# A hybrid decoder trunk on one core: the mixing stage in source order, taps on VectorE alone, seven W_out chunks open in PSUM

## The chip, the cores and the metric

The kernel runs on one core of a Trainium2 chip. The metric is the device time of one execution in microseconds. The engines are TensorE (PE, with its weight loads as PEld), VectorE (DVE), ScalarE (ACT), GpSimd (POOL) and SyncE (SP), which here only issues DMAs. Each engine and each DMA queue works off its own list of instructions in order.

## What is computed

Two layers over 512 positions of 1024 channels in float32; cut to what matters:

```python
def mixing_layer(h, ...):
    u = h @ w_in                       # 1024 -> 256+256+256+512+512+512+512
    a_b, a_c, a_x, q, k, v, c_in = split(u)
    y_a = a_b * causal_depthwise_conv(a_c * a_x, short_conv_w)        # 3 taps
    q, k = apply_rope(q), apply_rope(k)                                # 4 heads x 2 maps x 64
    o = diff_attention(q, k, v, lam)   # (softmax_1 - lam * softmax_2) v, causal
    y_b = rmsnorm(o, diff_subln_g) * (1.0 - lam_init)
    c = (c_in + glu_b); c = c[..., :256] * sigmoid(c[..., 256:])
    c = causal_depthwise_conv(c, conf_dw_w) + conf_dw_b                # 31 taps
    y_c = silu(layernorm(c, conf_ln_g, conf_ln_b))
    return concat([y_a, y_b, y_c]) @ w_out

for l in range(2):
    x = x + mixing_layer(rmsnorm(x, mix_norm_g[l]), ...)
    x = x + swiglu(rmsnorm(x, ffn_norm_g[l]), w_gate[l], w_up[l], w_down[l])   # hidden 2816
return rmsnorm(x, final_norm_g)
```

## The kernel before

The state `x` lies transposed in SBUF, as eight chunks of 128 channels x 512 positions. Every operand of a product is held as a rounded high part and a low part (fp32r), and a product is three matmuls, hi*hi, hi*lo and lo*hi (`mm3`, lines 152 to 154). The norm's scale `r` is applied after the projections, so that matmuls can start before it is known (`make_r`).

Weights come in units of eight 128x128 blocks (512 KB, 96 units a layer), in the order in which they are used. `prep` handles half a unit: the first half starts the unit's load on the SP queue (`raw`, two buffers), ACT makes the high part (line 125), and DVE or GpSimd subtracts it from the raw weights to get the low part (line 127; in the first 30 units of a layer two halves in three go to GpSimd). `next_half` prepares five halves ahead of the one in use; there are six tiles `w`.

The mixing stage of a layer: `conf_in` computes the gated columns `cc` (eight halves); `rotated(g, ...)` computes q and k of two heads (four units), rotates them with `cosr` and `sinr`, splits them and copies them with 64 KB DMAs on the SP queue into the packed tiles `pq`, `pk` (line 356): 16 copies for q and 32 for k of each pair of heads. `values` computes v for all heads into four PSUM banks (eight halves), and ACT evacuates it (`vt`, line 370). `Head.weigh` computes the scores of one block of 128 queries in both maps, their maxima (line 399), exponentials (line 401) and their combination (lines 404 to 406); `turn` transposes it through PSUM (line 416) and ACT copies it (line 418); `values` multiplies it with v (line 430); `finish` normalizes and transposes a head. `conf_conv` does the 31 taps of two chunks: 23 as one DVE operation each (lines 483 and 485), eight as a product on ACT and an addition on GpSimd (lines 488 to 493). `short_conv` is the gated convolution, `conf_out` the LayerNorm with its Silu. `stream` multiplies with W_out in two passes: first six of the eight inputs, then the last two (`YORDER`, `YCUT`), each pass adding its eight output chunks to `x`; the second pass also makes the next `h` and the sum of squares.

The order of the instructions of every engine and of SP's DMAs is chosen by the framework's planner from the program and its estimated times, not by the source: the source's order is a priority.

Of the kernel before, what the change touches and what calls it, by code (L numbers as in the profile page):

```python
# [43 lines left out]
POOL_TAPS = 8  # L44
# [11 lines left out]
YORDER = [6, 7, 2, 3, 0, 1, 4, 5]  # L56
YCUT = 6
# [17 lines left out]
def trunk(ctx, tc, xT, pos, wu, cv, lamv, cst, out):  # L75
# [13 lines left out]
    pc = pool("pc", 3)  # L89
# [3 lines left out]
    sc = pool("sc", 4, space=PSUM)  # L93
# [13 lines left out]
    def prep(i):  # L107

        if i >= 2 * L * UNITS or i in wtiles:
            return  # L110
        u, half = divmod(i, 2)
        if u not in wraw:
            wraw[u] = pw.tile([P, 2, 4 * P], F32, tag="raw", name=f"raw{u}", bufs=2)
            if u:
                nc.sync.dma_start(wraw[u].rearrange("p a b -> p (a b)"), wu[u])
            else:
                for j in range(2):
                    nc.sync.dma_start(wraw[u][:, j, :], wu[u, :, 4 * P * j:4 * P * j + 4 * P])
                    if j == 0:
                        nc.sync.dma_start(x[0], xT[0])  # L120
                        nc.sync.dma_start(cvt, cv)
# [46 lines left out]
    def four(name):  # L168
        return [sc.tile([P, S], F32, tag="sc", name=f"{name}{i}") for i in range(4)]
# [17 lines left out]
    prep(0)  # L187
    for k in range(1, KC):
        nc.sync.dma_start(x[k], xT[k])
        if k % 2 and k + 1 < AHEAD:  # L190
            prep(k)
            prep(k + 1)
    for i in range(1, AHEAD):
        prep(i)
# [25 lines left out]
    def add_square(k, run, eng):  # L220
        if k == 0:
            run = pt.tile([P, S], F32, tag="t", name="run")
            A.activation(run, x[0], AF.Square)
            return run
        sq = pt.tile([P, S], F32, tag="t", name="sq")
        A.activation(sq, x[k], AF.Square)
        (V if k == KC - 1 else eng).tensor_add(run, run, sq)
        return run
# [19 lines left out]
    def scale_of(parts, mul, eps, key, pool, ptag, n=4):  # L248
# [22 lines left out]
        if n < 4:  # L271
            dgs = [(diag(pe, a, F32, "at", V, bufs=3), ones_d)]
# [12 lines left out]
    def make_r(run):  # L285
        y, pb = scale_of([run], 1.0, RMS_EPS, "r", tp, "tp")
        rT = sm.tile([P, 4], F32, tag="rT", name="rT", bufs=2)
        V.tensor_scalar(rT, y, RQ, None, ALU.mult)
        r = cp.tile([P, S], F32, tag="r", name="r")
        A.copy(r, pb)  # L290
        return r, rT


    def rope_tables():
        p1, p2, p3 = _parts()
        pi = pt.tile([P, P], I32, tag="t", name="posi")
        A.dma_start(pi, pos)
# [19 lines left out]
        for b in range(4):  # L317
            A.dma_start(dr[:, :, b, :], tab[32 * b:32 * b + 32, :, :])
# [3 lines left out]
    def rotated(g, h, cosr, sinr):  # L322
# [3 lines left out]
        packs = []  # L326
        for isk in (False, True):
            ps = [unit(h, "qk") for _ in range(2)]
            t = [pt.tile([P, S], F32, tag="t", name=f"ro{i}") for i in range(4)]
            V.tensor_mul(t[0], ps[0], cosr)  # L330
            V.tensor_mul(t[1], ps[0], sinr)
            V.tensor_mul(t[2], ps[1], sinr)
            V.tensor_mul(t[3], ps[1], cosr)
            V.tensor_sub(t[0], t[0], t[2])
            V.tensor_add(t[1], t[1], t[3])
            for ab in range(2):
                o = t[ab]
                hl = pr.tile([P, 2, S], F32R, tag="hl", name="hl")
                if isk:
                    A.copy(hl[:, 0, :], o)  # L340
                    V.tensor_sub(hl[:, 1, :], o, hl[:, 0, :].bitcast(F32))
                else:
                    A.mul(hl[:, 0, :], o, QS)
                    V.scalar_tensor_tensor(hl[:, 1, :], o, QS, hl[:, 0, :].bitcast(F32), ALU.mult, ALU.subtract)
                if not packs:
                    packs += [[pk.tile([P, 2, S], F32R, tag=tag, name="p" + tag) for tag in ("q", "k1", "k2")]
                              for _ in range(2)]
# [9 lines left out]
        return packs  # L357

    def values(h, rT):
        ws = four("v")  # L360
        for k, b, w in side_by_side(3):
# [3 lines left out]
            T.matmul(ws[b], lhsT=h[k][:, 1, t], rhs=w[:, 0, :], start=False, stop=k == KC - 1)  # L365
        vt = []
# [7 lines left out]
    class Head:  # L374


        def __init__(self, hh, packs, nlam, gsub):
            self.hh, self.packs, self.nlam, self.gsub = hh, packs, nlam, gsub
            self.lsum = sm.tile([P, 2, 4], F32, tag="lsum", name="lsum")
            self.ss = sm.tile([P, 4], F32, tag="ss", name="ss")  # L380
            self.e, self.at = {}, {}
            self.o = self.raw = None

        def weigh(self, qb):

            q, k1, k2 = self.packs
            lsum = self.lsum
            n = (qb + 1) * P
            qs = slice(qb * P, n)
            e = []  # L390
            pss = [sc.tile([P, S], F32, tag="sc", name="ps") for _ in range(2)]
            for m in range(2):
                T.matmul(pss[m][:, :n], lhsT=q[:, m, qs], rhs=k1[:, m, :n], start=True, stop=False)
                T.matmul(pss[m][:, :n], lhsT=q[:, m, qs], rhs=k2[:, m, :n], start=False, stop=False)
                T.matmul(pss[m][:, qs], lhsT=idr, rhs=maskr, start=False, stop=True)
            for m in range(2):
                ps = pss[m]
                nm = sm.tile([P, 1], F32, tag="nm", name="nm")
                V.tensor_reduce(nm, ps[:, :n], AX.X, ALU.max, negate=True)
                t = pe.tile([P, S], F32, tag="e", name="e")  # L400
                A.activation(t[:, :n], ps[:, :n], AF.Exp, bias=nm, accum_out=lsum[:, m, qb:qb + 1])
                e.append(t)
            c = sm.tile([P, 1], F32, tag="c", name="c")
            V.reciprocal(c, lsum[:, 1, qb:qb + 1])
            V.tensor_scalar(c, c, lsum[:, 0, qb:qb + 1], self.nlam, ALU.mult, ALU.mult)
            V.scalar_tensor_tensor(e[0][:, :n], e[1][:, :n], c, e[0][:, :n], ALU.mult, ALU.add)
            self.e[qb] = e[0]

        def turn(self, qb):

            n = (qb + 1) * P
            e = self.e.pop(qb)
            pT = tp.tile([P, S], F32, tag="tp", name="pT")
            for kb in range(qb + 1):
                ks = slice(kb * P, kb * P + P)
                T.transpose(pT[:, ks], e[:, ks], ident)
            at = pe.tile([P, S], F32, tag="at", name="at", bufs=3)
            A.copy(at[:, :n], pT[:, :n])
            self.at[qb] = at

        def values(self, qb, vt):
            if qb == 0:
                self.o = av.tile([P, 4, P], F32, tag="av", name="o")
                self.raw = pe.tile([P, 4, P], F32, tag="os", name="os", bufs=2)
            o = self.o[:, qb, :]
            at = self.at.pop(qb)
            es = slice(self.hh * P, self.hh * P + P)
            for kb in range(qb + 1):
                ks = slice(kb * P, kb * P + P)
                T.matmul(o, lhsT=at[:, ks], rhs=vt[kb][:, es], start=kb == 0, stop=kb == qb)  # L430
            junk = sm.tile([P, P], mybir.dt.bfloat16, tag="junk", name="junk", bufs=1)
            A.activation(junk, o, AF.Square, accum_out=self.ss[:, qb:qb + 1])
            A.copy(self.raw[:, qb, :], o)

        def finish(self):

            e1 = sm.tile([P, 4], F32, tag="e1", name="e1")
# [3 lines left out]
            y0 = rsqrt(e1, 4, "h")  # L441
            raw = self.raw
            for qb in range(4):
# [406 lines left out]
```

## Time and profile before

| | us |
|---|---|
| median of 3 runs (1200.77 to 1202.13) | 1200.81 |
| the profiled execution | 1200.55 |
| its span, from first to last instruction | 1198.4 |
| PE busy in the span | 1146.2 |
| DVE busy in the span | 702.3 |
| mean granted TensorE clock, as a share of full speed | 0.981 |

A duration in the profile includes an instruction's way through the engine. Matmuls overlap: one of 128x512 is shown with 0.39 us, though the next one starts 0.227 us later; so a stage is measured by starts, idle time and granted clock. "idle before" in a row is the engine's idle time ahead of that instruction, with the instruction that ended it.

### The profile page before, as it was taken

To read this page: it belongs to the slowest core of one execution; us is meant where nothing else is said; L and a number is where in the kernel's file an instruction comes from. 1 tells how busy PE (TensorE), PEld (TensorE's weight loads), DVE (VectorE), ACT (ScalarE), POOL (GpSimd) and SP (SyncE) were. 2 spreads that over 40 slices of the span, in tenths; PEclk is the share of its full clock that TensorE was granted. 3 is DMA by queue.
4 is the path that set the end of the run, shared out by engine and by line. 5 is a ranking of instruction groups with operands and counts; after the bars stand their busy time and mean duration, and the time that the engine had idled before them with its cause. 6 is when DMAs were issued, how large, how long until landed. Compare 5 with 4: busy or idle time off the path is not lost.

```text
span 1198.4 us, 14491 instructions
## 1 busy us (share of the span) xinstructions
PE 1146.2 (96%) x5238; PEld 944.9 (79%) x5238; DVE 702.3 (59%) x1228; ACT 482.4 (40%) x960; POOL 268.6 (22%) x197
## 2 busy tenths in 40 slices
PE   8887999999999999999999799899999999999996
PEld 6666887778888888888887588787888888888885
DVE  7899976664443344444459997848544433444435
ACT  6534465443332233333353354735433222333323
POOL 3545323211110010110335553222111000111001
PEclk9897999999999999999999899999999999999998
DMA  5443532223232323232223344222232323232322
GB/s 188 131 103 113 134 115 86 73 89 106 89 105 90 104 90 104 90 104 90 104 88 112 99 136 116 81 73 88 88 106 88 106 88 106 88 106 88 106 71 71
DMA packets 42343, 120.19 MB, mean 100 GB/s; under 512 B 6816, under 2 KB 9760, under 8 KB 42272
## 3 DMA queue, kind: packets, MB, share of 16 engines
q1 hardware_dynamic: 40896, 117.77, 30.7%
q10 hardware_dynamic: 1376, 1.51, 0.6%
q8 instruction: 41, 0.67, 0.2%
q14 instruction: 30, 0.25, 0.1%
HBM read 104.44 MB, written 2.23 MB: 89 GB/s over the span
## 4 chain that ended last, share of the span: by engine, by line
PE 81%; DVE 13%; ACT 3%; DMA 1%; issue 1%; SPq 0%; ACTq 0%; DVEq 0%
PE od L153 8%; PE od L154 8%; PE od L152 8%; PE gp L152 7%; PE gp L153 7%; PE gp L154 7%; PE up L153 7%; PE up L154 6%; PE up L152 6%; DVE acc L485 6%; PE o L430 2%; DVE w L127 1%; PE qk L154 1%; PE qk L152 1%; PE qk L153 1%
## 5 line engine op out<-in xcount | busy, mean ns | idle before, releaser
L125 ACT CAST w<-raw 128x512 fp32r<-128x512 f32 x384 | 235.9, 621 | 519.6 <-PE od L154 175.9
L127 DVE TENSOR_TENSOR w<-raw,w 128x512 fp32r<-128x512 f32 x304 | 225.2, 741 | 250.3 <-ACT w L125 249.3
L731 POOL TENSOR_TENSOR tg<-tg,r 128x512 f32<-128x512 f32 x44 | 56.7, 1291 | 525.6 <-ACT tg L730 516.0
L127 POOL TENSOR_TENSOR w<-raw,w 128x512 fp32r<-128x512 f32 x80 | 116.7, 1466 | 188.0 <-ACT w L125 188.0
L153 PE MATMUL up<-h,w 128*128 128x512 f32 x352 | 137.6, 391 | 2.5 <-DVE h L217 2.5
L152 PE MATMUL gp<-h,w 128*128 128x512 f32 x352 | 137.1, 390 | 0.0
L153 PE MATMUL gp<-h,w 128*128 128x512 f32 x352 | 137.0, 389 | 0.0
L154 PE MATMUL gp<-h,w 128*128 128x512 f32 x352 | 137.0, 389 | 0.0
L154 PE MATMUL up<-h,w 128*128 128x512 f32 x352 | 137.0, 389 | 0.0
L152 PE MATMUL up<-h,w 128*128 128x512 f32 x352 | 136.9, 389 | 0.0
L152 PE MATMUL od<-act,w 128*128 128x512 f32 x328 | 127.6, 389 | 0.0
L153 PE MATMUL od<-act,w 128*128 128x512 f32 x328 | 127.6, 389 | 0.0
L154 PE MATMUL od<-act,w 128*128 128x512 f32 x328 | 127.6, 389 | 0.0
L485 DVE SCALAR_TENSOR_TENSOR acc<-pad,cvt,acc 128x503 f32<-128x503 f32 (+10 forms) x88 | 90.6, 1030 | 1.6
L153 PEld LDWEIGHTS up<-h,w 128*128 128x128 f32 x352 | 66.1, 188 | 17.6 <-DVE h L217 4.2
L152 PEld LDWEIGHTS gp<-h,w 128*128 128x128 f32 x352 | 66.1, 188 | 14.4 <-DVE x L705 0.6
L152 PEld LDWEIGHTS up<-h,w 128*128 128x128 f32 x352 | 66.0, 188 | 13.8
L154 PEld LDWEIGHTS gp<-h,w 128*128 128x128 f32 x352 | 66.0, 188 | 13.7
L153 PEld LDWEIGHTS gp<-h,w 128*128 128x128 f32 x352 | 66.1, 188 | 13.6
L154 PEld LDWEIGHTS up<-h,w 128*128 128x128 f32 x352 | 66.1, 188 | 13.5
L154 PEld LDWEIGHTS od<-act,w 128*128 128x128 f32 x328 | 61.6, 188 | 12.9
L152 PEld LDWEIGHTS od<-act,w 128*128 128x128 f32 x328 | 61.6, 188 | 12.8
(249 smaller groups left out, 2005.8 us busy)
## 6 DMA issues: line engine op xcount, KB each, us to landing
raw<-wu SPq DMA_DIRECT2D x191, 512.0 KB, 3.5
pk<-hl SPq DMA_DIRECT2D x128, 64.0 KB, 2.0
pq<-hl SPq DMA_DIRECT2D x64, 64.0 KB, 2.0
x<-xT SPq DMA_DIRECT2D x8, 256.0 KB, 6.4
yT<-fo SPq DMA_DIRECT2D x8, 256.0 KB, 2.3
raw<-wu SPq DMA_DIRECT2D x2, 256.0 KB, 3.3
cosr<-tab_dram ACTq DMA_DIRECT2D x8, 64.0 KB, 4.6
sinr<-tab_dram ACTq DMA_DIRECT2D x8, 64.0 KB, 3.6
```

Source lines behind the costliest of these rows:

```text
L125: A.copy(t[:, 0, :], raw)
L127: eng.tensor_sub(t[:, 1, :], raw, t[:, 0, :].bitcast(F32))
L152: T.matmul(ps, lhsT=hi, rhs=rh[:, 0, :], start=first, stop=False)
L153: T.matmul(ps, lhsT=hi, rhs=rh[:, 1, :], start=False, stop=False)
L154: T.matmul(ps, lhsT=lo, rhs=rh[:, 0, :], start=False, stop=last)
L430: T.matmul(o, lhsT=at[:, ks], rhs=vt[kb][:, es], start=kb == 0, stop=kb == qb)
L485: V.scalar_tensor_tensor(acc[:, d:], pad[:, :S - d], wt(d), acc[:, d:], ALU.mult, ALU.add)
L731: G.tensor_mul(t, t, r)
```

## The change

Each layer's mixing stage stands in one function, `mixing`, inside `tc.manual_schedule()`: in it every engine and queue issues its instructions in the order of the source. The q and k projections of the second pair and the gated convolution become a generator of steps of three matmuls (`steps_of`); two steps are put behind each block's scores and two behind its values, and more between the pairs (`fill`). Taps are handed out one by one (`tap`) and all run on DVE. The scores of both maps share a two-bank PSUM tile, one reduction finds both maxima, and the norm of two heads is made at once, with its scalings on ACT. Of the low parts, two halves in three of units 4 to 29 are made by ACT (the negated high part) and an accumulating DMA on GpSimd's queue that adds the raw weights from HBM; the others by DVE. Raw weights get three buffers and are loaded up to two units ahead. The rotation tables go over GpSimd's queue, and `rope_tables` and `lambdas` stand at the start. W_out is one pass: seven output chunks stay open in PSUM over four, then two, then the last two inputs; the eighth is done in one piece as the third to be finished (`DONE`). The factor `r` is applied in the gated convolution by DVE, squared (`r2`) in the first product.

```diff
-POOL_TAPS = 8
-YORDER = [6, 7, 2, 3, 0, 1, 4, 5]
-YCUT = 6
+YORDER = [0, 1, 2, 3, 4, 5, 6, 7]
+YA, YB = 4, 6
+OPEN = 7
+DONE = [0, 1, 7, 2, 3, 4, 5, 6]
...
-    sc = pool("sc", 4, space=PSUM)
+    sc = pool("sc", 2, space=PSUM)
...
+    def load(u):
+        if u in wraw or u >= L * UNITS:
+            return
+        wraw[u] = pw.tile([P, 2, 4 * P], F32, tag="raw", name=f"raw{u}", bufs=3)
...
+    def prep(i, ahead=True):
...
         u, half = divmod(i, 2)
+        load(u)
+        for k in range(1, 2 + half if ahead else 1):
+            load(u + k)
         raw = wraw[u][:, half, :]
...
         A.copy(t[:, 0, :], raw)
-        eng = G if (u % UNITS) < 30 and i % 3 else V
-        eng.tensor_sub(t[:, 1, :], raw, t[:, 0, :].bitcast(F32))
+        if 4 <= u % UNITS < 30 and i % 3:
+            A.mul(t[:, 1, :], raw, -1.0)
+            G.dma_start(t[:, 1, :], wu[u, :, 4 * P * half:4 * P * half + 4 * P], accum_op=ALU.add)
+        else:
+            V.tensor_sub(t[:, 1, :], raw, t[:, 0, :].bitcast(F32))
...
+    def qk_units(g, h, cosr, sinr, packs, between):
         for isk in (False, True):
-            ps = [unit(h, "qk") for _ in range(2)]
+            ps = acc.tile([P, S], F32, tag="acc", name="qk")
+            yield from steps_of(ps, h)
+            between(2 * isk)
...
-            V.tensor_mul(t[0], ps[0], cosr)
-            V.tensor_mul(t[1], ps[0], sinr)
-            V.tensor_mul(t[2], ps[1], sinr)
-            V.tensor_mul(t[3], ps[1], cosr)
+            V.tensor_mul(t[0], ps, cosr)
+            V.tensor_mul(t[1], ps, sinr)
+            ps = acc.tile([P, S], F32, tag="acc", name="qk")
+            yield from steps_of(ps, h)
+            between(2 * isk + 1)
+            V.tensor_mul(t[2], ps, sinr)
+            V.tensor_mul(t[3], ps, cosr)
             V.tensor_sub(t[0], t[0], t[2])
             V.tensor_add(t[1], t[1], t[3])
...
-    def values(h, rT):
+    def values(h, rT, each):
...
+            if n % 4 == 3:
+                each(n // 4)
...
+            nm = sm.tile([P, 2], F32, tag="nm2", name="nm")
+            V.tensor_reduce(nm, ps[:, :, :n], AX.X, ALU.max, negate=True)
...
+        def norm(self):
...
+            y0 = rsqrt(e1, 8, "h")
+            for b in range(8):
+                o = self.raw[b // 4][:, b % 4, :]
+                A.activation(o, o, AF.Copy, scale=y0[:, b:b + 1])
...
+    def mixing(l, h, run, tab, lams, each):
...
+        cc(24)
+        mr = make_r(run)
+        rT = next(mr)
...
+        cc(8)
+        r = next(mr)
+        pads = conf_gate(pp, r, cb)
...
+        for _ in qk_units(0, h, cosr, sinr, packs[0], lambda n: tap((0, 0, 1, 4)[n])):
+            pass
...
+        vt = values(h, rT, lambda n: tap((2, 2, 2, 2, 3, 3, 3, 3)[n]))
...
+        for b in range(8):
+            if b:
+                pairs[0].turn(b - 1)
+            pairs[0].scores(b)
+            fill(2)
+            tap(1)
+            pairs[0].weigh(b)
+            if b:
+                pairs[0].values(b - 1)
+            fill(2)
+        pairs[0].turn(7)
+        fill(4)
+        tap(3)
+        pairs[0].values(7)
+        fill(4)
+        pairs.append(Pair(1, packs[1], vt, nlam, gsub))
+        for b in range(8):
+            if b:
+                pairs[1].turn(b - 1)
+            pairs[1].scores(b)
+            fill(2)
+            tap(1)
+            pairs[1].weigh(b)
+            if b == 0:
+                pairs[0].norm()
+            elif b < 3:
+                y[1 + b] = pairs[0].finish(b - 1)
+            if b:
+                pairs[1].values(b - 1)
+            fill(2)
+        pairs[1].turn(7)
+        fill(4)
+        tap(2)
+        pairs[1].values(7)
+        fill(9)
+        pairs[1].norm()
...
+        for dc in range(OPEN):
+            grow(dc, 0, YA)
+            if dc in (1, 2):
+                y[3 + dc] = pairs[1].finish(dc - 1)
+            else:
+                tap(5)
+        tap(K31 * 2)
+        ln = conf_out(accs, cb)
+        next(ln)
+        for dc in range(OPEN):
+            grow(dc, YA, YB)
+            if dc in (0, 3):
+                next(ln)
+        y[6], y[7] = next(ln)
+        for dc in DONE:
+            if dc < OPEN:
+                grow(dc, YB, KC)
+            else:
+                od.append(acc.tile([P, S], F32, tag="acc", name="od7"))
+                grow(dc, 0, KC)
+            each(dc, od[dc])
...
+        with tc.manual_schedule():
+            mixing(l, h, run, tab, lambda l: (nlams[l], gsubs[l]), after_mix)
```

## Rows read from the trace of the kernel before

**Rows 1.** The page, part 1: busy time, share of the span, instructions.

```profile
PE 1146.2 (96%) x5238; PEld 944.9 (79%) x5238; DVE 702.3 (59%) x1228; ACT 482.4 (40%) x960; POOL 268.6 (22%) x197
```

**Rows 2.** Windows by stage: us, busy time of each engine, granted clock, DMA.

```profile
5.80:242.40 236.60, 214.31 (x993) 174.54 (x993) 196.41 (x365) 122.33 (x284) 97.75 (x68) 0.95 0.38 115
242.40:598.90 356.50, 356.50 (x1578) 295.30 (x1578) 157.16 (x239) 122.24 (x199) 41.62 (x32) 1.00 0.30 98
598.90:825.60 226.70, 209.82 (x993) 172.17 (x991) 181.99 (x333) 110.97 (x262) 92.89 (x62) 0.97 0.32 98
```

**Rows 3.** Timeline of PE where each mixing stage begins and ends.

```profile
5.79 0.50 PE L152 MATMUL cc<-h,w 128*128 128x512 f32 x1 [0.19 <-ACT h L216]
...
242.39 0.50 PE L152 MATMUL gp<-h,w 128*128 128x512 f32 x1
...
598.89 0.39 PE L152 MATMUL cc<-h,w 128*128 128x512 f32 x1
599.12 0.39 PE L153 MATMUL cc<-h,w 128*128 128x512 f32 x1
...
825.62 0.50 PE L152 MATMUL gp<-h,w 128*128 128x512 f32 x1
```

**Rows 4.** Windows of PE's waits in the first mixing stage, columns as above.

```profile
47.30:53.20 5.90, 5.90 (x14) 4.64 (x15) 5.90 (x7) 1.90 (x4) 5.80 (x5) 0.50 0.11 29
...
87.00:104.00 17.00, 8.25 (x29) 6.97 (x29) 16.72 (x28) 8.54 (x24) 9.60 (x8) 0.61 0.32 93
```

**Rows 5.** Timeline of the SP queue, 40 to 180 us: start, us, issues.

```profile
55.16 10.95 SPq L356 DMA_DIRECT2D pq<-hl  x16
...
70.57 20.55 SPq L356 DMA_DIRECT2D pk<-hl  x32
91.22 31.68 SPq L115 DMA_DIRECT2D raw<-wu  x7
```

**Rows 6.** Timeline of DVE: two neighbouring taps, one alone, one beside GpSimd.

```profile
92.93 0.72 DVE L485 SCALAR_TENSOR_TENSOR acc<-pad,cvt,acc 128x497 f32<-128x497 f32 x1
...
94.44 1.60 DVE L485 SCALAR_TENSOR_TENSOR acc<-pad,cvt,acc 128x496 f32<-128x496 f32 x1
```

**Rows 7.** Timeline of ACT: two high parts in a row.

```profile
102.29 1.14 ACT L125 CAST w<-raw 128x512 fp32r<-128x512 f32 x2
```

**Rows 8.** Landings: of the k copies (by tile), of the weight loads (page).

```profile
DMA to landing us min/median/max: 1.9/2.0/3.8
...
raw<-wu SPq DMA_DIRECT2D x191, 512.0 KB, 3.5
```

**Rows 9.** Groups by shape, first mixing stage: count, busy us, mean ns, idle before.

```profile
L330 DVE TENSOR_TENSOR ro<-qk,cosr 128x512 f32<-128x512 f32 x4 | 2.7, 679 | 0.0
...
L370 ACT ACTIVATE vt<-v,rT 128x512 f32<-128x512 f32 x4 | 2.7, 679 | 6.0 <-PE v L365 6.0
```

**Rows 10.** The same view: the operations between scores and transposes.

```profile
L399 DVE TENSOR_REDUCE nm<-ps 128x1 f32<-128x512 f32 x8 | 5.4, 680 | 0.7 <-PE ps L395 0.7
L399 DVE TENSOR_REDUCE nm<-ps 128x1 f32<-128x128 f32 x8 | 2.2, 277 | 0.2 <-PE ps L395 0.2
...
L401 ACT ACTIVATE e<-ps,nm 128x384 f32<-128x384 f32 x8 | 4.7, 588 | 6.5 <-DVE e L406 4.4 <-DVE rqln L245 1.5 <-DVE nm L399 0.5
...
L404 DVE RECIPROCAL c<-lsum 128x1 f32<-128x1 f32 x16 | 2.5, 154 | 1.3 <-ACT e L401 1.1
L405 DVE TENSOR_SCALAR c<-c,lsum,nlam 128x1 f32<-128x1 f32 x16 | 4.2, 266 | 0.2
...
L406 DVE SCALAR_TENSOR_TENSOR e<-e,c 128x384 f32<-128x384 f32 x4 | 2.5, 613 | 0.1
```

**Rows 11.** The same view: the end of the LayerNorm.

```profile
L521 ACT ACTIVATE acc<-acc,cvt 128x512 f32<-128x512 f32 x2 | 1.5, 810 | 0.0
...
L524 DVE TENSOR_TENSOR yc<-acc,yc 128x512 fp32r<-128x512 f32 x2 | 1.5, 737 | 0.0
```

More of the change, by code (lines that the diff above doesn't have):

```diff
@@ L168, in four @@
     def four(name):
-        return [sc.tile([P, S], F32, tag="sc", name=f"{name}{i}") for i in range(4)]
+        ps = [sc.tile([P, 2, S], F32, tag="sc", name=f"{name}{i}") for i in range(2)]
+        return [ps[i // 2][:, i % 2, :] for i in range(4)]
     def unit(h, name, pool=None):
@@ L190, in trunk @@
         if k % 2 and k + 1 < AHEAD:
[L191 to L194, printed above, removed]
+            prep(k, False)
+            prep(k + 1, False)
     ones_d = cp.tile([P, P], F32, name="ones_d")
@@ L226, in add_square @@
         A.activation(sq, x[k], AF.Square)
-        (V if k == KC - 1 else eng).tensor_add(run, run, sq)
+        (V if (k == KC - 1 if last is None else last) else eng).tensor_add(run, run, sq)
         return run
@@ L334, in rotated @@
+            V.tensor_mul(t[3], ps, cosr)
             V.tensor_sub(t[0], t[0], t[2])
             V.tensor_add(t[1], t[1], t[3])
+            if not packs:
+                packs += [[pk.tile([P, 2, S], F32R, tag=tag, name="p" + tag) for tag in ("q", "k1", "k2")]
+                          for _ in range(2)]
+            hls = [pr.tile([P, 2, S], F32R, tag="hl", name="hl") for _ in range(2)]
             for ab in range(2):
-                o = t[ab]
-                hl = pr.tile([P, 2, S], F32R, tag="hl", name="hl")
@@ L406, in weigh, with turn @@
             V.scalar_tensor_tensor(e[0][:, :n], e[1][:, :n], c, e[0][:, :n], ALU.mult, ALU.add)
[L407 to L412, printed above, removed]
+        def turn(self, b):
+            n = (b % 4 + 1) * P
+            e = self.e.pop(b)[0]
             pT = tp.tile([P, S], F32, tag="tp", name="pT")
+            for kb in range(b % 4 + 1):
+                ks = slice(kb * P, kb * P + P)
+                T.transpose(pT[:, ks], e[:, ks], ident)
+            at = pe.tile([P, S], F32, tag="at", name="at", bufs=2)
+            A.copy(at[:, :n], pT[:, :n])
+            self.at[b] = at
@@ L417, in turn @@
[L417 to L430, printed above, removed]
+                T.matmul(o, lhsT=at[:, ks], rhs=self.vt[kb][:, es], start=kb == 0, stop=kb == qb)
@@ L510, in conf_out @@
         yield
-        st = scale_of([sq[0]], 4.0, LN_EPS, "ln", acc, "acc")
+        st = scale_of([sq[0]], 4.0, LN_EPS, "ln", tp, "tp")
         next(st)
         yield
-        rs = pt.tile([P, S], F32, tag="t", name="lnr")
-        A.copy(rs, next(st))
+        rb = next(st)
         ys = []
@@ L532, in wt, with new @@
             return cvt[:, c:c + 1]
-        ps = unit(h, "ax")
+        def new(name):
+            return acc.tile([P, S], F32, tag="acc", name=name)
+        ps = new("ax")
+        yield from steps_of(ps, h)
         t = pt.tile([P, S], F32, tag="t", name="tx")
-        V.tensor_mul(t, ps, r)
-        G.tensor_mul(t, t, r)
-        yield
-        ps = unit(h, "ac")
+        V.tensor_mul(t, ps, r2)
+        ps = new("ac")
+        yield from steps_of(ps, h)
         V.tensor_mul(t, ps, t)
@@ L543, in short_conv @@
             V.scalar_tensor_tensor(a[:, d:], t[:, :S - d], wt(d), a[:, d:], ALU.mult, ALU.add)
-        G.tensor_mul(a, a, r)
-        yield
-        ps = unit(h, "ab")
+        V.tensor_mul(a, a, r)
+        ps = new("ab")
+        yield from steps_of(ps, h)
         V.tensor_mul(a, ps, a)
-        y = py.tile([P, 2, S], F32R, tag="ya", name="ya")
-        A.copy(y[:, 0, :], a)
-        V.tensor_sub(y[:, 1, :], a, y[:, 0, :].bitcast(F32))
-        yield y
+        ya = py.tile([P, 2, S], F32R, tag="ya", name="ya")
```

308 lines of the change are left out of this document (152 added, 156 removed).

## Prediction, made before the changed kernel was run

> **What bounds the kernel now.** First the page's busy shares: TensorE (PE) is busy 96% of the span, VectorE (DVE) 59% [rows 1]. No engine but PE can set the whole; where PE is not busy is the question. The windows by stage answer it [rows 2]: in the FFN between the layers PE has no idle time at a granted clock of 1.00. The mixing stages lose time: the first lasts from the first cc matmul to the first gp matmul, 236.6 us, the second 226.7 [rows 2, 3]. In them PE is idle for 236.60 - 214.31 = 22.3 and 226.70 - 209.82 = 16.9 us, and clocks of 0.95 and 0.97 take another 11.8 and 6.8 at most (half of the two clock levels, 1.2 instead of 2.4 GHz, for a part of the stage). What is left is PE's own work: 202.5 and 203.0, so about 203 us a stage. A change of the mixing stages can win 60 us at most, and what it wins depends on how many of the new order's waits fall on PE.
>
> Where did PE wait? In 87 to 104 us it is busy for 8.3 of 17 us at a clock of 0.61 [rows 4]. The SP queue explains it: the 16 copies that bring q into its packed tile take 10.95 us to issue, the 32 copies of k 20.55, about 0.64 each, and the next weight load starts only behind them, at 91.22 [rows 5]. VectorE's taps are slow there as well: one takes 0.72 alone and 1.60 beside GpSimd [rows 6].
>
> **The change, part by part.** I call a weight tile a half: four 128x128 blocks, 12 matmuls at 0.227 us start to start [rows 3], 2.72 us of PE. Of a layer, halves 0 to 7 are cc, 8 to 15 q and k of the first pair of heads, 16 to 23 the values, 24 to 31 q and k of the second pair, 32 to 43 the gated convolution, 44 to 59 W_out. PE's matmuls stay the same in number, 203 us.
>
> *Taps, low halves, sums.* 62 taps a layer at 0.72 are 44.6 us of DVE; the 44 of before took about as much, since many of them met GpSimd [rows 6]. Eight x additions fewer (the two W_out passes become one), sixteen scalings moved to ScalarE (ACT), 16 reductions' starts less and a few more low halves on DVE nearly cancel. ACT gets some 35 negations of 0.57 [rows 7] and loses 16 tap products. Both engines stay below PE over the stage (DVE has 196 busy us in 236.6 now [rows 2], contention included), so I cost these at nothing by themselves: PE covers them. Without that cover, where one engine's instructions stand in a row ahead of something PE needs, they are in the terms below.
>
> *Low halves by accumulating DMA.* No row shows such a DMA. Half i is prepared when half i-5 begins, 13.6 us ahead. A plain load of 512 KB lands in 3.5 us [rows 8]; negation and landing would have to take four times that to be seen. I take nothing; the other end is a rival.
>
> *Term 1, the loads behind the copies.* All queues run in source order, SP's too. The load of unit u (halves 2u and 2u+1) is now issued when half 2u-8 begins, and ACT needs it when half 2u-5 begins: 8.2 us. But the q copies stand ahead of unit 10's load and the k copies ahead of unit 12's. Count from the first q matmul of the first pair. The second unit ends at 4 x 2.72 = 10.9; three DVE operations of 0.68 and a cast of 0.57 [rows 7, 9] later, at 13.5, the first copy goes; sixteen at 0.64 end at 23.7; unit 10 lands 3.5 later [rows 8], at 27.2. ACT stands before half 20 from 19.1 on. With that half's two ACT operations and the k cast behind it, the k copies start at 28.9, 7.1 after q and k end on PE (21.8, called T). They end at T+27.6 and unit 12 lands at T+31.1. ACT then has the eight casts and negations of halves 24 to 28 (4.6) and two evacuations of the values (0.68 each [rows 9]) before the scores' PSUM tile is free: T+37.1. PE ends the values at T+21.8. That is 15.3 us without work; DVE, held by half 24's low half, has 14 taps (10 us) left ahead of the first maximum, up to 3 more. If the k copies started at T+3, 11 would remain. I take 16 (11 to 19).
>
> *Term 2, the second pair's k.* Its last k matmul is the last filler of block 7. Behind it three DVE operations and a cast, 2.6, then the copies; the first score needs the 20th (12.2 later) and its landing, 2.0 [rows 8]: 16.8, the second half of the scores the 24th, 19.3. PE has in between eight filler steps (24 matmuls, 5.4) and 12 small matmuls, each below 0.227: 5.4 to 8.2. The wait is 8.6 to 13.9; I take 11.5. Today short convolutions lie there, in an order the planner chose; in source order they stand behind the scores.
>
> *Term 3, the clock.* After an idle stretch of 3.2 us the next 5.9 us ran at 0.50, 14 matmuls at twice their time [rows 4]: 2.9 lost. Terms 1 and 2 make two longer stretches a stage, at places where PE then waits anyway. I take 3 (0 to 6).
>
> *Term 4, the blocks.* Between a block's scores and its transposes lie, for 384 keys, a maximum over both maps (0.134 for each 128 elements and 0.14 [rows 10]: 0.95), two exponentials of 0.59, and 0.15 + 0.27 + 0.61 on DVE [rows 10]: 3.2 us. PE's cover is four filler steps, 2.72, and up to 0.9 of values: about even. But DVE runs the fillers' work between maximum and combination: after each unit two products (1.4), after each second one four operations, two casts and two low halves (4.2), in the gated convolution chains of 3.4 and 2.0; and the first pair's norm puts eight scalings ahead of the copy that block 1 needs. The exponentials hide 1.2 of each. Over 16 blocks I count 1, 2.5, 1 in the first pair and 3, 3, 0.5 in the second: 11 (5 to 16).
>
> *Term 5, the end.* The LayerNorm's two chunks come last and nothing else stands behind them on PE: product 0.68, Silu 0.81, cast 0.57, the second pair of them behind, low half 0.74 [rows 7, 9, 11]: 3.3 beyond PE's own 1.4; the gated convolution's second chunk is about 1.2 late at the first chunk of W_out. 4.5 (2 to 6). Seven open chunks cover the norm's statistics (six matmuls each).
>
> Sum: 16 + 11.5 + 3 + 11 + 4.5 = 46; a stage 203 + 46 = 249, two 498 against 236.6 + 226.7 = 463.3: +34.7. The profiled execution took 1200.55 us, 2.15 beyond its span and 0.26 under the median shown, so I use it as it is: 1235. All lower ends (26.6) give 1196, all upper ends (60.9) 1265.
>
> **The rivals.** *A: the copies do not hold PE.* Then terms 1 to 3 fall away: 203 + 15.5 = 218.5 a stage, 437 in all, 1174: faster. It decides as soon as terms 1 to 3 together stay below 13 us a stage, for 203 + 15.5 + 13.2 is the present mean of 231.7. It would be so if a copy were issued in under a third of its 0.64, or if loads and copies didn't stand in one line. Against it: 0.64 in both rows of copies and the load behind them [rows 5]; for it: the loads now start two units ahead with three buffers. The Trainium skill ("DMA: Bandwidth & Descriptors", Issuing engines are not separate DMA queues) says that the time to initiate a DMA on a sequencer is usually small relative to the DMA itself. By that rule this rival holds. The trace does not agree for a row of 32: one is issued in 0.64 and lands in 2.0 [rows 5, 8], ten landings' time in the row.
>
> *B: the accumulating DMAs come late.* PE would stop at two halves in three. For 1 us over the cover at each of some 35 a stage it is 70 us in all, of which the waits above hide a part: around 1275. For it speaks only that no row shows one. The same skill page (Anatomy of one DMA) has for GpSimd's DMAs 2.0 us and the bytes at 436 GB/s, 2.6 us for 256 KB, as an estimate; by that the sum stays.
>
> *C: no change.* Term 1 exists today in another form (87 to 104 us), and shorter taps may shorten term 4: with all lower ends the stages come out within 5 us of today's.
>
> **How the numbers follow.** Forecast 0.61, A 0.22, B 0.08, C 0.09. Faster by over 0.2% (2.4 us, about what this kernel's runs can tell from no change) is A with 0.21 and C with 0.04: 0.25. Within it lie 0.01 of A, 0.03 of C and 0.02 of the forecast's low end: 0.06. Slower are the forecast's other 0.59, B and 0.02 of C: 0.69. The likeliest case's own range is 1203 to 1262; for 8 in 10 it has to reach into A, whose lower half and B stay out: 1182 to 1262.
>
> **What would show it.** After: SP's timeline with 32 k copies of some 20 us and a weight load behind them; PE's waits at the first scores of each pair (ps), some 10 us or more each, ended by ACT's vt or by the copies; taps at 0.72 throughout; POOL nearly empty in the stage. I am wrong if PE passes from the values to the scores and from pair to pair with waits of a few us, or if the stage windows fall below 225 us.

## The result: 1319.8 us, 118 us slower, and the profile after

The changed kernel takes 1319.83 us (median of 4, 1319.31 to 1324.57) beside 1201.47 for the kernel before: ratio 1.0993, 95% interval 1.0966 to 1.102. The direction was the forecast one; the size was not. 1235 was predicted, with 1262 as the upper end of the range. The profiled execution took 1324.57, the slowest of the four.

The page's part 1 of the changed kernel answers to [rows 1]. PE has the same 5238 matmuls, and is shown busy for 35 us more (one of 128x512 is shown with 0.63 where the granted clock is 0.50, with 0.39 at 1.00):

```profile
PE 1181.7 (89%) x5238; PEld 965.4 (73%) x5238; DVE 644.0 (49%) x1152; ACT 502.2 (38%) x1025; POOL 159.3 (12%) x168
```

The windows by stage, columns as in [rows 2], from the first cc matmul to the first gp matmul and on to the next layer:

```profile
6.61:292.07 285.46, 220.78 (x950) 176.17 (x951) 159.29 (x316) 128.13 (x307) 39.25 (x51) 0.87 0.50 124
292.07:660.18 368.11, 366.47 (x1620) 303.13 (x1619) 166.39 (x252) 127.09 (x209) 42.62 (x33) 1.00 0.29 96
660.18:937.40 277.22, 218.47 (x952) 175.12 (x951) 144.57 (x281) 115.41 (x285) 35.48 (x44) 0.87 0.47 113
937.40:1322.60 385.20, 371.48 (x1711) 309.64 (x1709) 172.50 (x298) 128.73 (x222) 41.01 (x35) 0.98 0.28 91
```

The boundary has shifted: 42 matmuls that stood ahead of the first gp (993 there before, 951 now) now come behind it, so the FFN windows are some 12 us longer, 9.5 of them these matmuls' own time (42 x 0.227). Whole layers compare cleanly: 653.6 and 662.4 us against 593.1 and 599.4, which is +60.5 and +63.0. The stage windows show two kinds of loss. PE is idle for 285.46 - 220.78 = 64.7 and for 58.8 us (22.3 and 16.9 before), and the granted clock is 0.87 in both (0.95 and 0.97 before).

Who ended PE's waits in the first stage (engine, what waited, for whom: us in total, times, longest):

```profile
PE pT L453 <- DVE e L444: 21.9, 9, 11.2
PE ps L426 <- ACT vt L404: 12.4, 1, 12.4
PE ps L426 <- DMA pk<-hl: 7.0, 2, 6.4
PE ssps L267 <- issue: 6.5, 1, 6.5
PE pT L453 <- DVE yb L491: 5.0, 2, 3.9
PE od L165 <- ACT yc L550: 4.8, 2, 3.9
PE v L396 <- DMA w<-wu: 3.2, 3, 1.4
```

Four single waits stand out: 12.4 at the first pair's first scores (Term 1 foresaw it), 6.4 at the second pair's scores (Term 2), 6.5 at the norm's sums (`ssps`, first layer only; the profile shows nothing that PE waited for there), and 11.2 at the transposes of the first pair's last block. The prediction had neither of the last two. SP's timeline shows where the wait of 11.2 begins:

```profile
54.04 10.93 SPq L389 DMA_DIRECT2D pq<-hl  x16
65.02 1.08 SPq L115 DMA_DIRECT2D raw<-wu  x2
70.54 22.11 SPq L389 DMA_DIRECT2D pk<-hl  x32
92.70 18.96 SPq L115 DMA_DIRECT2D raw<-wu  x6
132.21 23.09 SPq L389 DMA_DIRECT2D pq<-hl  x16
155.35 1.08 SPq L115 DMA_DIRECT2D raw<-wu  x2
164.86 20.17 SPq L389 DMA_DIRECT2D pk<-hl  x32
```

The first pair's 16 q copies take 10.93 us, the second pair's 23.09. After four of them SP stops. The queue's own waits name what it waits for, and the timelines of ACT, DVE and PE show who pays:

```profile
SPq L389 <- PE ps L428: 13.1, 1, 13.1
```

```profile
150.32 0.20 ACT L434 ACTIVATION_READ_ACCUMULATOR e<-ps,nm 128x1 f32 x1
159.22 0.62 ACT L135 CAST w<-raw 128x512 fp32r<-128x512 f32 x1 [8.70 <-DMA raw<-wu]
```

```profile
159.87 0.69 DVE L140 TENSOR_TENSOR w<-raw,w 128x512 fp32r<-128x512 f32 x1 [10.83 <-ACT w L135]
...
161.64 0.75 DVE L444 SCALAR_TENSOR_TENSOR e<-e,c 128x512 f32<-128x512 f32 x1
```

```profile
162.54 1.09 PE L453 MATMUL pT<-idr,e 128*128 128x128 f32 x4 [11.24 <-DVE e L444]
```

There are two packed tiles `pq`, so that of the second pair's second head is the one that the first pair's second head still reads, up to its last scores at 147.6. Its copies wait for that; the weight load of 155.35 waits behind them; ACT stands before the cast of these weights until 159.22; and the low part, a tap and the combination (line 444) stand behind that cast on DVE, the transposes behind the combination on PE.

### The profile page after: what moved, and what is told of

It reads as the page before. It is cut to its first block, busy times and chain, and to the rows that moved or that the text cites. A ratio compares the mean times of both kernels' runs of the same rounds, so it can differ in the third digit from the quotient of the medians.

```text
span 1322.7 us, 14441 instructions
## 1 busy us (share of the span) xinstructions
PE 1181.7 (89%) x5238; PEld 965.4 (73%) x5238; DVE 644.0 (49%) x1152; ACT 502.2 (38%) x1025; POOL 159.3 (12%) x168
## 4 chain that ended last, share of the span: by engine, by line
PE 74%; DVE 10%; SPq 6%; ACT 5%; DMA 2%; issue 2%; DVEq 0%; ACTq 0%
PE od L166 8%; PE od L165 8%; PE od L167 8%; PE up L165 6%; PE gp L165 6%; PE up L167 6%; PE up L166 6%; PE gp L166 6%; PE gp L167 6%; SPq L389 6%; DVE acc L521 3%; DMA raw<-wu 2%; DVE nm L430 1%; ACT e L434 1%; PE cc L166 1%
## 5 line engine op out<-in xcount | busy, mean ns | idle before, releaser
L138 POOL DMA_DIRECT2D w<-wu x70 | 60.1, 858 | 450.4 <-ACT w L137 317.4
L521 DVE SCALAR_TENSOR_TENSOR acc<-pad,cvt,acc 128x511 f32<-128x511 f32 (+14 forms) x120 | 88.0, 733 | 2.6
L166 PEld LDWEIGHTS gp<-h,w 128*128 128x128 f32 x352 | 66.1, 188 | 13.5
```

The lines of the kernel that those rows point to most:

```text
L138: G.dma_start(t[:, 1, :], wu[u, :, 4 * P * half:4 * P * half + 4 * P], accum_op=ALU.add)
L166: T.matmul(ps, lhsT=hi, rhs=rh[:, 1, :], start=False, stop=False)
L521: V.scalar_tensor_tensor(a[:, d:], pad[:, :S - d], cvt[:, c - d:c - d + 1], a[:, d:], ALU.mult, ALU.add)
```

## The experiments

Each kernel is the changed one with the edit shown, if nothing else is said. Differences are of medians; the medians of the kernel before, measured again beside them, lie between 1201.4 and 1202.1. The range behind a ratio is its 95% interval.

**Is it the order?** The planner gets the mixing stage back; all else is as changed.

```diff
-        with tc.manual_schedule():
-            mixing(l, h, run, ...)
+        if True:
+            mixing(l, h, run, ...)
```

> The changed kernel with the same source, but its mixing stage ordered by the planner instead of by the source. If the fixed order is the cause of the +119 us (theory), the planner puts ready matmuls and ready loads into the waits, PE's idle time of 65 and 59 us a stage falls to about the 22 and 17 of the kernel before, and the time comes to 1190 to 1215. If the changed work itself costs the time (the one pass over W_out, the accumulating DMAs, all taps on VectorE), the time stays above 1250 in any order.

1201.90 us, ratio to before 0.9999 (0.9977 to 1.0022). The same work in a free order takes no longer than before, so the whole loss is order. Its windows:

```profile
5.80:236.10 230.30, 207.81 (x974) 171.14 (x975) 156.99 (x322) 130.06 (x312) 44.29 (x60) 0.96 0.63 158
598.70:819.90 221.20, 205.95 (x976) 170.22 (x976) 140.34 (x287) 117.82 (x288) 32.38 (x37) 0.96 0.59 140
```

**Does the half clock cost time?** Slices of 1 us show ten stretches at a clock of 0.50 in the first stage, 75 us in all. Busy time in a slice, times what is missing of the clock, sums to 24.3 us of lost work (8.8 before), and to 22.8 in the second stage (5.9). These matmuls keep PE at work where it waits:

```diff
+        def idle(n):
+            d = tp.tile([P, S], F32, tag="tp", name="dm")
+            for _ in range(n):
+                T.matmul(d, lhsT=ones_r, rhs=h[0][:, 0, :], start=True, stop=True)
...
+        if l == 0:
+            idle(25)
...
+        idle(50)
         pairs = [Pair(0, packs[0], vt, nlam, gsub)]
...
+        idle(45)
         pairs[0].turn(7)
...
+        idle(25)
```

> The changed kernel with matmuls that compute nothing used in PE's longest waits: 50 ahead of the first pair's scores (a wait of 12.4 us, 50 x 0.227 = 11.4), 45 ahead of the last transposes of the first pair (11.2), 25 ahead of the second pair's scores (6.4), 25 ahead of the norm's sums in the first layer (6.5). What PE waits for is untouched. If the half clock behind these waits costs what the windows show (3.2 + 1.7 + 2.0 + 3.6 us of work a stage, 3.2 more in the first), the clock stays at 1.00 there and the time falls by up to 24, to 1296 to 1310; if the slower matmuls there lie in waits for other engines anyway, it stays at 1316 to 1323; if the added matmuls outlast the waits, it is above 1323.

1321.12 us, ratio to before 1.0983 (1.0958 to 1.1007): the same as the changed kernel. The span's mean clock rose from 0.940 to 0.976, and the lost work fell from 24.3 to 10.5 and from 22.8 to 14.1 us. None of it came back as time. PE's timeline shows why:

```profile
84.16 11.49 PE L589 MATMUL dm<-h,ones_r 128*128 128x512 f32 x50
99.00 0.33 PE L426 MATMUL ps<-pk,pq 128*128 128x128 f32 x1 [3.35 <-ACT vt L404]
...
108.21 0.45 PE L453 MATMUL pT<-idr,e 128*128 128x128 f32 x1 [5.50 <-DVE e L444]
```

The scores still wait for ACT's `vt` (11.49 us of filling and 3.35 idle); the matmuls behind them run at full speed, and PE then waits longer for the combination, 5.5 us instead of 2.4. Idle time and filling together (265 matmuls at 0.227) are some 17 us longer in the two stages than the idle time was: most of the restored work went into longer waits. The Trainium skill ("TensorE: Matmul & The Clock Gate", Why this matters for your kernels) advises against idle gaps between bursts of matmuls, for the clock. The clock does follow that advice here; the time does not.

**What does the packed tile cost?** Its eight q copies are issued behind the scores that still read it.

```diff
+                                if late is not None and hh and not isk:
+                                    late.append(io)
+                                else:
+                                    nc.sync.dma_start(*io)
...
             pairs[0].scores(b)
+            if b == 7:
+                for io in late:
+                    nc.sync.dma_start(*io)
```

> The changed kernel with eight of the second pair's 16 q copies (those into the packed tile of its second head, which the first pair's last scores still read) issued behind these scores, so that SP does not stand before them with weight loads behind. If this buffer wait is what starves ACT and leaves PE idle for 11.2 us before the first pair's last transposes, that idle time falls below 3 and the time falls by 10 to 13 a layer, to 1293 to 1300. If the wait only moves to the copies of k, PE waits as much longer at the second pair's scores and the time stays above 1312.

1304.91 us (ratio to before 1.0848, 1.0822 to 1.0874), 15 less: 7.5 a layer, between the two expectations. PE's waits in its first stage:

```profile
PE pT L457 <- DVE e L448: 13.2, 9, 2.7
...
PE ps L430 <- DMA pk<-hl: 9.7, 2, 9.1
```

The wait of 11.2 is gone (the longest of its kind is 2.7), and the copies of k, now next in line, hold the second pair's scores for 9.1 instead of 6.4.

**What do SP's rows cost?** The second head's copies go over GpSimd's queue; then, in the second of these runs, also head by head, with the late q copies of the run before.

```diff
-                                nc.sync.dma_start(to[dst:dst + 32, m, :]...
+                                (G if hh else nc.sync).dma_start(to[dst:dst + 32, m, :]...
```

> The changed kernel with the copies into the packed tiles of each pair's second head on GpSimd's queue, half of all 96 a layer; the first head's stay on SP. If SP's rows of copies with a weight load behind them set the stage's pace (rows of 11 and 22 us, halved here; the packed tile that is still read no longer blocks SP), the wait of 12.4 us at the first scores falls to 1 to 3, that of 11.2 at the end of the first pair goes, and the time falls by 10 to 20 a layer, to 1280 to 1300. If a copy is dear on GpSimd's queue, or the accumulating DMAs stand behind the packed tile there instead, PE waits for w in their place and the time stays above 1305.

1290.84 us (1.0742, 1.0716 to 1.0768), 29 less, as expected. GpSimd's queue now stands before the packed tile that is still read:

```profile
137.86 3.99 POOL L389 DMA_DIRECT2D pq<-hl  x8 [18.06 <-PE ps L428]
```

> As the run with the second head's copies on GpSimd's queue, and besides the copies go head by head (the first scores need 16 of k on SP, all of the first head), and the second pair's q copies into the tile that is still read are issued behind the first pair's last scores. No queue then waits for a buffer. By the theory of the queues 22 to 30 a layer go (12.4, 11.2 and 6.4 us of waits, less what is left of each), to 1260 to 1276; if the waits only move to the chains of the blocks, above 1290.

1290.65 us (1.0743, 1.0725 to 1.076): no more than that, not the 1260 to 1276 that were expected, though the late copies wait only 1.2 us for their packed tile now instead of 18.1. The two edits weren't run apart, but by this such a wait need not cost anything by itself; on SP the weight loads stood behind it. Three of PE's long waits in its first stage are shorter than in the changed kernel (1.8 at the first scores, 2.7 at transposes, 4.2 at the second pair's scores), but the one for low parts has grown from 3.2, and GpSimd's timeline explains it:

```profile
65.99 3.80 POOL L395 DMA_DIRECT2D pk<-hl  x7
70.17 0.50 POOL L395 DMA_DIRECT2D pk<-hl  x1 [0.38 <-DMA w<-wu]
71.03 3.92 POOL L395 DMA_DIRECT2D pk<-hl  x8 [0.35 <-issue]
75.16 1.81 POOL L138 DMA_DIRECT2D w<-wu  x2 [0.21 <-DMA pk<-hl]
```

```profile
PE v L402 <- DMA w<-wu: 7.8, 2, 4.0
```

The accumulating DMAs stand behind the copies, as the weight loads did on SP. So the low parts that fall in that time go to DVE:

```diff
-        if 4 <= u % UNITS < 30 and i % 3:
+        if (4 <= u % UNITS < 6 or 13 <= u % UNITS < 30) and i % 3:
```

> The run with copies on two queues, head by head, and the low parts of units 6 to 12 on VectorE instead of the accumulating DMA. In that run PE waits 7.8 and 9.6 us a stage in the values for a low part whose DMA stands behind 16 copies on GpSimd's queue. If that is the whole of this wait, it goes and the time falls by 6 to 9 a layer, to 1272 to 1279; if the weights or VectorE set the same moment, less than 3 a layer.

1277.77 us (1.0633, 1.0611 to 1.0655), 13 less, as expected.

**What stands between a block's maximum and its combination?** DVE's timeline of the changed kernel, one block: seven operations of the fillers and a tap stand inside, from 129.64 to 134.67, 5.0 us:

```profile
129.30 0.42 DVE L430 TENSOR_REDUCE nm<-ps 128x2 f32<-128x256 f32 x1 [1.43 <-PE ps L428]
129.64 0.68 DVE L362 TENSOR_TENSOR ro<-qk,sinr 128x512 f32<-128x512 f32 x1
...
133.43 0.68 DVE L140 TENSOR_TENSOR w<-raw,w 128x512 fp32r<-128x512 f32 x1
134.03 0.72 DVE L521 SCALAR_TENSOR_TENSOR acc<-pad,cvt,acc 128x483 f32<-128x483 f32 x1
134.67 0.16 DVE L442 RECIPROCAL c<-lsum 128x1 f32<-128x1 f32 x1
...
135.17 0.35 DVE L444 SCALAR_TENSOR_TENSOR e<-e,c 128x128 f32<-128x128 f32 x1
```

In both pairs the combination goes ahead of the fillers:

```diff
             pairs[0].scores(b)
+            pairs[0].weigh(b)
             fill(2)
             tap(1)
-            pairs[0].weigh(b)
```

> The changed kernel with each block's combination (its three VectorE operations) put ahead of the two filler steps and the tap that stood between the maximum and it; the tap comes behind. If the fillers' operations and the tap in that place make PE wait at the transposes (22 us of waits in the first stage, 11.2 of them the block with the late weights), the waits of 2.4 to 3.9 fall to under 1.5 and the time falls by 6 to 10 a layer, to 1300 to 1308. If VectorE, which then stands before the exponentials, makes the fillers late in their place, it stays at 1315 to 1325.

1308.88 us (1.089, 1.0868 to 1.0912), 11 less, just above the first expectation. The waits for `e` fall from 21.9 to 7.9 in the first stage, but the wait for late weights shows up as others (rows of its waits, first stage):

```profile
PE ps L426 <- ACT vt L404: 13.4, 1, 13.4
PE ps L426 <- DMA pk<-hl: 11.0, 2, 10.4
PE pT L453 <- DVE e L444: 7.9, 9, 2.7
...
PE o L468 <- ACT at L455: 6.0, 2, 5.5
```

> The last run and the one with the combination ahead of the fillers together: if the two waits are independent, the gains add to 12 to 19 a layer under the run with two queues, to 1253 to 1267; if one hides behind the other, no better than the better of the two.

1266.20 us (1.0532, 1.0513 to 1.0551), 11.6 under the run before it: the two gains add.

**Where do taps cost?** 14 taps leave the values for the blocks, where each block has two instead of one.

```diff
-        vt = values(h, rT, lambda n: tap((2, 2, 2, 2, 3, 3, 3, 3)[n]))
+        vt = values(h, rT, lambda n: tap((2, 2, 2, 0, 0, 0, 0, 0)[n]))
...
-            tap(1)
+            tap(2)
```

> The changed kernel with 14 of the 20 taps that stand between the values' halves moved behind the scores, two a block instead of one. If VectorE's row of taps ahead of the first maximum is what holds the first pair's start (it ends about 109 us, the scores' matmuls at 108), the first maximum comes 3 to 5 us earlier and the time falls by 3 to 4 a layer, to 1311 to 1315. If the wait behind it (the late weights) takes its place, or the second tap a block costs as much, it stays at 1317 to 1323.

1334.91 us (1.1112, 1.1093 to 1.113), 15 more, outside both expectations: what the first block won, 16 taps a stage ahead of the combination lost again and more. With the copies on two queues as well:

> The last run with the 14 taps moved as well. With the weights early, VectorE's row of taps is what stands ahead of the first maximum; moved, 2 to 4 us a layer less than the last run. If the taps are behind nothing that PE needs then, no difference over 2.

1304.18 us (1.0855, 1.0838 to 1.0871), 13.5 above that run: the expectation was wrong here too.

**Does the clock bind once the queues are quieter?** Matmuls that compute nothing again, in the run of 1266.20 us.

> The run of 1266 us (copies on two queues, low parts of units 6 to 12 on VectorE, combination ahead of the fillers) with matmuls that compute nothing used in what is left of PE's longest waits: 20 at the norm's sums of the first layer, 16 ahead of each pair's first scores. With the queues' waits shorter, the half clock behind them (2.9, 2.3 + 2.4 and 3.5 us of work in the first stage) may bind now: then 4 to 8 a layer less, to 1250 to 1258. If the waits for VectorE, ACT and the copies take it up again, as they did in the changed kernel itself, it stays within 3 of 1266.

1264.83 us (1.0519, 1.0489 to 1.0548), 1.4 less, which is within the spread of its runs (1262.7 to 1268.5). Some 7 us of lost work are restored in the two stages (15.7 to 10.0 and 11.9 to 10.2), so the clock binds by little, if at all.

**All such measures together,** on the run of 1266.20 us; the first pair's `norm` and `finish` also go ahead of the fillers.

```diff
-                                    (G if hh else nc.sync).dma_start(*io)
+                                    G.dma_start(*io)
...
-        if (4 <= u % UNITS < 6 or 13 <= u % UNITS < 30) and i % 3:
+        if False:
...
         pairs[0].values(7)
-        fill(4)
+        fill(8)
```

> The changed kernel with all copies on GpSimd's queue, head by head (0.50 each there, 0.63 on SP), the second pair's q into the tile still read behind the first pair's last scores, all low parts on VectorE, the combination ahead of the fillers, the first pair's finish ahead of them too, and four filler steps more between the pairs. SP then holds weight loads alone. Against the 1266 us of the run that it builds on: the wait of 5 us ahead of the first scores, 3 of 4 at the first transposes, 4.8 at the finish and 5 of 10 at the second pair's scores should go: 14 to 17 a layer, to 1232 to 1242. If VectorE, with all low parts, becomes late for the blocks, it stays above 1255.

1254.16 us (1.0431, 1.0407 to 1.0456), 12 less instead of 24 to 34. In the first stage the waits at the scores shrank (5.0 to 1.2 in the first pair, some 10 to 5.0 in the second). Those around the finish did not, 7.1 before and 9.2 now: they went in part from the blocks' transposes to its own. At the first transposes 4.7 stayed (DVE runs nine taps in a row, 6.85 us, ahead of the first maximum), and at the first chunk of W_out that needs `ya`, the gated convolution's result, 0.8 became 3.1; no run shows why.

> The run of 1254 us with the same 14 taps moved from the values to the blocks as in the run that got 15 us slower by it; here they stand behind the combination. If a tap costs PE time by its place in the chain from the maximum to the transposes, they are free now, the wait of 4.7 us at the first transposes falls to 1 to 2, and the time falls by 2 to 4 a layer, to 1246 to 1250. If VectorE's time in the blocks is what counts, wherever the tap stands, the time rises again by 8 to 15, above 1262.

1258.81 us (1.0475, 1.0455 to 1.0495), 4.7 more, between the two expectations. The wait of 4.7 is gone and the later blocks' waits have grown by as much: behind the combination 16 taps more a stage cost 4.7 us, about a third of the 13.5 to 15 ahead of it, not nothing.

> The last run, and in the first layer the norm's six sums for r stand behind all of cc instead of behind three quarters, and r behind the first unit of q. PE waits there for 6.3 us for the sum of squares (in the first layer only). If the place in PE's order makes this wait, it falls to 1 to 2, PE then waits up to 2.6 for the first unit's PSUM, and the time falls by 2 to 5. If the sum is late for whatever stands first, no difference over 1.

1255.28 us (1.0444, 1.0426 to 1.0462), 3.5 less than that.

**What are the change's parts worth in a free order?** In the kernel before, all taps go to DVE (`POOL_TAPS = 0`), then all low parts too, then the second head's copies to GpSimd's queue.

> The kernel before with all 31 taps on VectorE, and nothing else changed. If VectorE has room under PE (196 busy of 237 us, a part of it slowed by GpSimd), the time stays within 4 us of 1201; if VectorE becomes late for what PE needs, it is above 1207; if fewer slowed operations shorten the chains, below 1196.

1197.24 us, ratio 0.9961 (0.9945 to 0.9977), at the lower edge of the first expectation.

```diff
-        eng = G if (u % UNITS) < 30 and i % 3 else V
-        eng.tensor_sub(t[:, 1, :], raw, t[:, 0, :].bitcast(F32))
+        V.tensor_sub(t[:, 1, :], raw, t[:, 0, :].bitcast(F32))
```

> The kernel before with all taps on VectorE (0.4% faster than before) and all low parts on VectorE too, so that GpSimd leaves it alone. If GpSimd's remaining subtractions slow VectorE where PE waits for it, 3 to 8 us less than with the taps alone, 1189 to 1194; if VectorE has too much to do by then, above 1200.

1192.82 us, ratio 0.9921 (0.99 to 0.9941): it beats both kernels.

> The kernel before, ordered by the planner, with all taps and all low parts on VectorE, and the copies of each pair's second head on GpSimd's queue, which is empty in that stage now. If the rows of copies ahead of a weight load cost the planner's order too (8.7 us of idle time and a clock of 0.61 in its stretch of 87 to 104 us), the time falls to 1180 to 1188; if the planner has other work there, it stays at 1191 to 1195.

1191.91 us, ratio 0.9909 (0.9878 to 0.9941): no different. The expectation's reason for that, other work of the planner's there, isn't borne out: PE waits 8.2 us at the first stage's scores for copies of k, and 5.7 in the run of 1192.82. Why moving half of the copies leaves this wait, no run shows.

> The changed kernel ordered by the planner, with the copies of each pair's second head on GpSimd's queue and all low parts on VectorE. If the change's other parts (blocks of both maps at once, one pass over W_out, fillers) are worth something once the order is free, it comes below the kernel before with the same two measures; else it is equal or above, 1185 to 1200.

1197.17 us, ratio 0.9957 (0.994 to 0.9974): above the kernel before with the same two measures, so the change's other parts win nothing in a free order.

## Why the prediction was right in direction and wrong in size

*Term 1, the loads behind the copies (16, 11 to 19): right.* The k copies started 8.4 us after q and k ended on PE (predicted 7.1), took 22.11 (20.5), the load behind them landed 34.4 after (31.1), the first scores began 40.0 after (37.1). PE stood still for 12.4 us there and, earlier, for 3.2 in the values (for low parts whose negation on ACT came late). Moving half of the copies away gave back 29 us in the two layers, the second pair's share included. (The rows that the prediction read have 0.68 us a copy for q, 10.95 for 16, and 0.64 only for k; it changes little.)

*Term 2, the second pair's k (11.5, 8.6 to 13.9): nearly right as far as it went, with a step missing beside it.* The scores waited for the k copies for 7.0 us, and their second half for 1.4 more. But the prediction says nothing of the second pair's q copies, though two tiles `pq` serve four heads: SP waited 13.1 us for the first pair's last scores, and with it the loads, ACT and DVE. That is PE's unpredicted wait of 11.2 a stage; without it 15 us come back in the two layers.

*Term 3, the clock (3, 0 to 6): wrong by the profile, and not a term at all.* The windows show 24 and 23 us of lost work a stage. With 22.5 us of that restored the time didn't move, and with 7 restored in the run with quieter queues it moved by 1.4, within the spread. What set PE's progress was the next thing that it waited for, and slow matmuls ahead of a wait only fill it. In the record of one run idle time and lost work add up; as prices they don't, since each was measured in the other's presence.

*Term 4, the blocks (11, 5 to 16): at the upper end.* Without the 11.2, PE waited 15.7 us at the transposes of the first stage (21.9 + 5.0 - 11.2). Fillers and tap ahead of the combination cost 11 to 12 us in the two layers.

*Term 5, the end (4.5): right,* 5.8 at W_out.

*Costed at nothing.* The accumulating DMAs: nearly right as the kernel stood (the 3.2 us in the values; they landed in 4.9 us, not in the estimated 2.6), so rival B fell, until copies shared their queue (7.8 and 9.6). The taps: in a free order they win 0.4%, and in the fixed order 16 more a stage ahead of the combination cost 15 us, about 0.5 each: DVE had room over the stage, but not in the chain. The prediction had this rule in its text ("where one engine's instructions stand in a row ahead of something PE needs") and counted the taps of the values only. The first layer's 6.5 us at the norm's sums, placed after three quarters of cc in the source, were not foreseen; placed later, 3.5 came back.

*The sum.* Its idle part was 43 a stage; the windows have 64.7 and 58.8. The missed buffer wait (11.2), Term 4's excess (about 5) and the first layer's sums (6.5) are nearly that difference: 22.4 of 21.7 in the first stage, 15.9 of 15.8 in the second, Terms 1, 2 and 5 missing by little. The rest of the miss shows as slower matmuls, and by the runs these have no price of their own. So the step that failed is "Sum: 16 + 11.5 + 3 + 11 + 4.5 = 46": beside it the profile has 64.7 + 24.3 = 89 us in the first stage and 58.8 + 22.8 = 82 in the second, and even all upper ends (60.9) stay below. Taking the mean clock's 11.8 and 6.8 us off PE's own work made the 203 ahead of the sum up to 3 too small as well: by the slices the half clock took 8.8 and 5.9. It lacks the wait for the packed tile, and it takes each wait by itself, while in the rows from 132 to 163 us one late load stalls ACT, ACT's next cast DVE, and DVE's combination PE. Of the 85 us between 1235 and 1319.8 the runs price the packed tile at 15 and, in the kernel of 1258.8, the first layer's sums at 3.5; for the rest the cause stays open.

*Rivals.* A (copies don't hold PE) is refuted by the 29 us. The Trainium skill ("DMA: Bandwidth & Descriptors", Issuing engines are not separate DMA queues) says that issuing from several engines saves only the sequencer's time, usually small. Here that time was the cost: 32 copies took 22.11 us to issue, and a load stood behind them.

*What stays open.* Edits within the fixed order took 1319.8 to 1254.2, 66 of the 118 us; the free order takes it to 1201.9. In the last 52 the profile shows many waits of 0.5 to 6 us (41 and 31 us of idle time a stage are left, 22.3 and 16.9 before) and lost work of 14.9 and 12.1 (8.8 and 5.9 before). No edit that was tried removes them.

## What to carry to other kernels

When a planner's order is replaced by the source's, walk down every queue, SP's and GpSimd's included, and ask of each instruction what it waits for, buffers that are still read among them, and what stands behind it: a copy that waits for a tile takes the weight loads with it. Put what the next stage waits for first (the combination, then the fillers), and count an engine's room between two points of the chain, not over the stage. Before a low clock is blamed, fill the waits with matmuls that compute nothing and see whether the time moves.

## What the runs showed of the hardware that was not expected

A 64 KB copy between SBUF tiles is issued in some 0.50 us on GpSimd's queue (3.92 for 8 in the rows above) and in 0.63 on SP's (20.17 for the 32 of the second pair's k). An accumulating DMA of 256 KB landed in 4.9 us (median of 70), a plain load of 512 KB in 3.5.

DVE's taps get shorter as GpSimd's additions and subtractions in the mixing stage go. The groups of taps (count, busy us, mean ns) of the kernel before, of it with all taps on DVE, and of it with all low parts there too:

```profile
L485 DVE SCALAR_TENSOR_TENSOR acc<-pad,cvt,acc 128x503 f32<-128x503 f32 (+10 forms) x88 | 90.6, 1030 | 1.6
```

```profile
L485 DVE SCALAR_TENSOR_TENSOR acc<-pad,cvt,acc 128x511 f32<-128x511 f32 (+14 forms) x120 | 105.6, 880 | 1.8
```

```profile
L484 DVE SCALAR_TENSOR_TENSOR acc<-pad,cvt,acc 128x511 f32<-128x511 f32 (+14 forms) x120 | 87.5, 729 | 1.3
```

With 32 taps more, DVE spends less on them. The Trainium skill ("GPSIMD Engine Reference", Key points) has the two share their SBUF interfaces, with contention for operations of two SBUF inputs; the trace agrees: 1030 ns a tap with GpSimd's taps and subtractions, 729 without either.
